# Reordering the second layer of a two-layer decoder step: memory attention first, one state tile for each pair of heads, eleven gate blocks last

## The chip, the cores and the metric

The kernel runs on one core of one Trainium2 chip. The metric is the device time of one execution in microseconds. Engines are named as in the profile: PE is the matrix engine (PEld its weight loads), DVE the vector engine, ACT the scalar engine, POOL and SP issue transfers.

## What is computed

One inference step of two layers for 256 prompt tokens and 8 sample tokens (264 columns), model width 2048. Each layer has one input projection that feeds a token mixer, four memory-attention heads and a gate; then an output projection and a LayerNorm.

```python
# layer 1: sliding-window attention; layer 2: HGRN2 recurrence, 12 heads of 128 x 128
fg = lb + (1 - lb) * sigmoid(f); qh = silu(q); kh = 1 - fg; vh = iv
o, s_new = hgrn2_chunked(qh, kh, vh, log(fg), s0)     # prompt: s0 = 0; samples: s0 = state_hgrn
o = o * rsqrt(mean(o*o, -1) + eps) * norm_w
mem_o = softmax(mq @ mk.T * 128**-0.5) @ mv           # 256 memory rows; samples have their own cached mk, mv
branch = concat([o, mem_o], -1) * silu(g)
x = LN(alpha * x + branch @ w_out)
# outputs: y of both groups, memory keys and values, window caches, final states (prompt and sample)
```

## The kernel before, in words

Everything that is streamed comes as blocks of 128x2048 numbers in f32 (1 MB): a projection's 2048x128 weight block, a memory cache of two samples, a state. `Stream` holds a list of units, one for each block, in an order written out in the code. A block is loaded by SP into a tile `raw` (four buffers), split by ACT (high f16 part, line 97) and DVE (low f16 part, line 98) into a tile `hl` (four buffers), up to three units ahead of its use, and then used by PE. `proj` multiplies a block in 48 passes: for each of 16 chunks high by high, high by low, low by high (`passes`, lines 303 to 305), into one of two PSUM banks `pj`. Smaller products use two banks `pt`, two `sc`, one `pv`, one `ms`.

In the second layer the units of a pair of heads `pi` are f, f, v, v, then for each head q, the head's state (512 KB, `state_unit`) and, for heads 0 to 7, its gate. After the twelve heads come the four memory queries `mq`, the eight memory caches (`ck_unit`, `cv_unit`) in turn with gates 8 to 13, gates 14 and 15, and sixteen blocks of the output projection (`o`). Gates of heads 0 to 7 (`early_gate`) wait in `mix` for their head; the others (`gate_unit`) are finished by `gate_fin` two gates later.

The prompt side of a pair is a generator, `hg_side`, of ten steps: seven levels of products (`hs`), each prepared by ACT and DVE, then the transposed keys (`pk` to `kn`), the states (`pu` to `s1`, `s2`), the outputs (`hpo` to `osb`), squares, `rms`, logarithm, exponential, and the scaling into `mix`. Pair n+1 uses the same buffers `st` and `prod` as pair n. `pump(1)` after every unit runs one step of the generator at the head of a queue; `drain()` ahead of the output projection runs what is left.

`state_unit` reads the split state for the eight samples (`hos`), then updates the f32 state in place in its `raw` tile: for each sample ACT scales (`raw <- raw, fg`, line 1237), PE spreads the value row over the partitions (`vb`, two `pt` banks of four samples each, from `vr` and a selector), DVE adds the product with the key column (line 1238); POOL writes the tile out.

The order in which each engine executes is fixed when the program is built: a scheduler puts every instruction into its engine's list by a timeline of its own, preferring what was written first. On the chip each engine takes its list from the top.

Of the kernel before, what the change touches and what calls it, by code (L numbers as in the profile page):

```python
# [21 lines left out]
TS = 8  # L22
# [11 lines left out]
NG1 = 8  # L34
# [12 lines left out]
LEVELS = (1, 2, 4, 8, 16, 32, 64)  # L47
NMASK = (len(LEVELS) - 1) * 64
# [9 lines left out]
class Stream:  # L58


    def __init__(self, nc, pool, nraw, nsplit):
        self.nc, self.pool = nc, pool
        self.nraw, self.nsplit = nraw, nsplit
        self.units = []
        self.raw = {}
        self.hl = {}

# [37 lines left out]
    def run(self, pump):  # L105
# [11 lines left out]
        for i in range(n):  # L117
# [8 lines left out]
            while free < prepped and (free <= i or self.units[free][5]):  # L126
                free += 1
# [7 lines left out]
def trunk_kernel(  # L135
# [75 lines left out]
    bias_s = pm.tile([P, 2, NQ], F32, name="bias_s")  # L211

# [94 lines left out]
    def proj(hl, src, n, name, cols=slice(None), tag="pj"):  # L307
# [77 lines left out]
    def q_unit(j):  # L385
        def fn(hl):
            load_bias(j)
            load_bias(j + 1)
            pt = proj(hl, xhl, T, f"q{j}")
# [326 lines left out]

    fin = {0: deque(), 1: deque()}
# [14 lines left out]
    def silu2(out, pt):  # L732
        nc.scalar.activation(out, pt, AF.Tanh, scale=0.5 * CP)
        nc.vector.scalar_tensor_tensor(out, out, 1.0, pt, op0=ALU.add, op1=ALU.mult)
# [10 lines left out]
    def residual(l, i, cols, n, pt):  # L745
        z = xres[:, i, cols]
        summed = nc.vector.scalar_tensor_tensor(z, z, ALPHA / CP, pt, op0=ALU.mult, op1=ALU.add)  # L747
# [235 lines left out]
    def f_unit(h):  # L983
        def fn(hl):
# [4 lines left out]
            pt = proj(hl, xhl, T, f"f{h}")  # L989
            i = h % 2  # L990
            if i == 0:
# [3 lines left out]
                cur["ks8"] = p1.tile([P, 2, TS], F32, tag="ks8", name=f"ks8{h}", bufs=2)  # L995
            fg, kk, ks8 = cur["fg"][:, i], cur["kk"][:, i], cur["ks8"][:, i]
# [6 lines left out]
            nc.vector.tensor_scalar_mul(ks8, kk, 1.0 / (SA * SK))  # L1003
# [5 lines left out]
    def hq_unit(h):  # L1009
        def fn(hl):  # L1010
# [5 lines left out]
            if h % 2 == 1:  # L1016
                side.append(hg_side(h // 2, cur["q"], cur["vn"], cur["fg"], cur["qk"]))
# [3 lines left out]
    later, due = [], []  # L1021

    def hv_unit(h):
        def fn(hl):
# [3 lines left out]
            if i == 0:  # L1028
                cur["vn"] = p1.tile([P, 2, 2, P], F32, tag="vn", name=f"vn{h}", bufs=2)
                cur["vr"] = p1.tile([P, 2, P], F16, tag="vr", name=f"vr{h}", bufs=2)  # L1030
# [10 lines left out]
    def hv_rows(h, vt, vs, vn, vr):  # L1041
# [7 lines left out]
        nc.vector.tensor_copy(vr[:, i], p16)  # L1049
# [14 lines left out]
    def hg_side(pi, q, vn, fg, qk):  # L1064
# [119 lines left out]
        for i, sq in enumerate(sqs):  # L1184
# [3 lines left out]
            scaled = mix[:, h] if h >= NG1 else sq  # L1188
# [3 lines left out]
            if h < NG1:  # L1192
# [4 lines left out]
    def state_unit(h):  # L1197
        def fn(hl):
            p1 = H["p"]
            pi, i = h // 2, h % 2  # L1200
            raw = stream.raw[state_at[h]][:, : TS * P]
            R = raw.rearrange("p (b v) -> p b v", b=TS)
            v = hl[:, :, : TS * P].rearrange("p s (b v) -> p s b v", b=TS)
            vr, fgs, ks8 = cur["vr"][:, i], cur["fg"][:, i, TP:T], cur["ks8"][:, i]
            qs, vts = (cur[n][:, i, TP:T] for n in ("q", "vt"))
            ks = cur["kk"][:, i]
            if i == 0:
                osb[pi] = p1.tile([P, 2, T], F32, tag="osb", name=f"osb{pi}", bufs=2)
            qk = p1.tile([P, TS], F32, tag="qk", name=f"qk{h}", bufs=2)
            qf = p1.tile([P, TS], F32, tag="qf", name=f"qf{h}", bufs=2)  # L1210
            qfh = p1.tile([P, TS, 2], F16, tag="qfh", name=f"qfh{h}", bufs=2)
            nc.vector.scalar_tensor_tensor(qf, qs, SA * 0.5 * CP, fgs, op0=ALU.mult, op1=ALU.mult)
            nc.vector.scalar_tensor_tensor(qk, qs, 8.0 * 0.5 * CP / SK, ks, op0=ALU.mult, op1=ALU.mult)
            qkh = p1.tile([P, 2, TS], F16, tag="qkh", name=f"qkh{h}", bufs=2)
            nc.scalar.activation(qkh[:, 0], qk, AF.Copy)
            nc.vector.tensor_tensor(qkh[:, 1], qk, qkh[:, 0], op=ALU.subtract)
            nc.scalar.activation(qfh[:, :, 0], qf, AF.Copy)
            nc.vector.tensor_tensor(qfh[:, :, 1], qf, qfh[:, :, 0], op=ALU.subtract)
            po = bank("ms", 1, f"hos{h}")
            pov = po[:, : 2 * TS].rearrange("p (b s) -> p b s", s=2)  # L1220
            for b in range(TS):
                mm(pov[:, b], v[:, 0, b], qfh[:, b], start=True, stop=False)
                mm(pov[:, b, 0:1], v[:, 1, b], qfh[:, b, 0:1], start=False, stop=True)
            pq = po[:, 2 * TS : 3 * TS]
            for s in range(2):
                mm(pq, H["ones"], qkh[:, s], start=s == 0, stop=s == 1)
            nc.vector.tensor_reduce(qf, pov, axis=AX.X, op=ALU.add)
            nc.vector.tensor_tensor(qk, pq, vts, op=ALU.mult)
            nc.vector.scalar_tensor_tensor(osb[pi][:, i, TP:T], qf, 1.0 / (SA * SA), qk, op0=ALU.mult, op1=ALU.add)
            for g in range(2):  # L1230
                pvb = bank("pt", 2, f"vb{h}{g}")
                for bb in range(4):
                    mm(pvb[:, bb * P : (bb + 1) * P], H["sel"][:, 4 * g + bb], vr, start=True, stop=True)
                for bb in range(4):
                    b = 4 * g + bb
                    s = R[:, b]
                    nc.scalar.activation(s, s, AF.Copy, scale=fgs[:, b : b + 1])
                    nc.vector.scalar_tensor_tensor(
                        s, pvb[:, bb * P : (bb + 1) * P], ks8[:, b : b + 1], s, op0=ALU.mult, op1=ALU.add
                    )  # L1240
# [192 lines left out]
```

## Time and profile before

| | |
|---|---|
| time, median of 3 runs | 906.81 us (906.51 to 907.01) |
| the profiled execution | 906.08 us, of which the span from first to last instruction is 904.3 us |
| PE busy | 886.6 us of the span (98%) |
| DVE, ACT busy | 701.5 us (78%), 582.4 us (64%) |
| granted PE clock, mean | 0.994 |
| second layer | from 420 us (first pass of `f`) to the end |

A row of a timeline gives the start, the duration, engine, line, operation, output <- inputs, shape, the number of such instructions, and in brackets how long the engine was idle before and what ended that. A row of a table of windows gives busy time (and count) of PE, PEld, DVE, ACT and POOL, the granted PE clock, and the share and rate of the transfers. A grouped row ends with busy time of the group, mean ns of one, and idle time before. PE's passes overlap in the records: one of 264 columns lasts 0.28 us and the next starts 0.11 us later.

### The profile page before, as it was taken

The page shows a single profiled execution, that of the slowest core. Times are in us where ns is not written, and L with a number is a line of the kernel's source. Part 1 is how long each engine was busy: PE and PEld are TensorE (multiplying, and loading weights), DVE is VectorE, ACT ScalarE, POOL GpSimd, SP SyncE. Part 2 cuts the span into 40 slices and gives each one's busy share as a digit, 9 for nine tenths or more (in the row PEclk, how much of TensorE's full clock was granted, in tenths as well). Part 3 has the DMA queues.
Part 4 walks back from the last instruction along what each step waited for, and adds up shares of the span by engine and source line. Part 5 has one row for each costly group of instructions (what it writes and reads, how often), then busy time and mean ns, then how long its engine had stood idle before and what let it go on. Part 6 is the DMA issues. An engine that isn't in the chain of part 4 may idle for free.

```text
span 904.3 us, 21814 instructions
## 1 busy us (share of the span) xinstructions
PE 886.6 (98%) x9281; PEld 762.9 (84%) x9281; DVE 701.5 (78%) x1230; ACT 582.4 (64%) x982; POOL 34.9 (4%) x68
## 2 busy tenths in 40 slices
PE   9999999999999999999999999999999999799996
PEld 6888889678888888876888888898888888688996
DVE  6879877669886666697687887979788989678736
ACT  6767776657664444476766877777777585858415
POOL 1100010000000000002000000000000000000000
PEclk9999999999999999999999999999999999899999
DMA  9998566557785555556374655827454878456303
GB/s 340 392 353 317 188 245 209 188 208 265 262 333 192 187 192 203 207 198 214 127 292 137 216 201 174 299 101 260 160 215 164 303 283 308 172 207 244 130 2 97
DMA packets 37853, 198.67 MB, mean 220 GB/s; under 512 B 4555, under 2 KB 10732, under 8 KB 17532
## 3 DMA queue, kind: packets, MB, share of 16 engines
q1 hardware_dynamic: 33024, 181.55, 56.3%
q0 software_dynamic: 4688, 15.67, 4.6%
q8 instruction: 72, 1.18, 0.5%
q14 instruction: 25, 0.20, 0.1%
q10 hardware_dynamic: 44, 0.07, 0.0%
HBM read 180.03 MB, written 17.22 MB: 218 GB/s over the span
## 4 chain that ended last, share of the span: by engine, by line
PE 77%; DVE 8%; ACT 6%; DMA 6%; issue 3%; SPq 0%; ACTq 0%; DVEq 0%
PE o L303 5%; PE o L305 5%; PE o L304 5%; PE g L305 5%; PE g L303 5%; PE g L304 5%; DVE hl L98 4%; ACT hl L97 2%; PE hv L305 2%; PE hv L303 2%; PE hv L304 2%; DMA raw<-in_w_in 2%; PE hq L303 2%; PE hq L305 2%; PE hq L304 2%
## 5 line engine op out<-in xcount | busy, mean ns | idle before, releaser
L98 DVE SCALAR_TENSOR_TENSOR hl<-raw,hl 128x2048 f16<-128x2048 f32 (+2 forms) x168 | 358.6, 2138 | 82.0 <-ACT hl L97 81.0
L97 ACT ACTIVATE hl<-raw 128x2048 f16<-128x2048 f32 (+2 forms) x168 | 299.2, 1784 | 97.8 <-PE o L305 45.4
L305 PEld LDWEIGHTS <-hl 128*128 128x128 f16 (+2 forms) x2048 | 197.4, 98 | 31.8 <-DVE hl L98 2.9
L303 PEld LDWEIGHTS <-hl 128*128 128x128 f16 (+2 forms) x2048 | 197.3, 98 | 30.6 <-issue 2.2
L304 PEld LDWEIGHTS <-hl 128*128 128x128 f16 (+2 forms) x2048 | 197.4, 98 | 30.3 <-issue 2.2
L305 PE MATMUL g<-xhl,hl 128*128 128x264 f16 x512 | 142.0, 277 | 2.4 <-DVE hl L98 2.4
L303 PE MATMUL g<-xhl,hl 128*128 128x264 f16 x512 | 141.9, 277 | 0.0
L304 PE MATMUL g<-xhl,hl 128*128 128x264 f16 x512 | 141.9, 277 | 0.0
L303 PE MATMUL o<-mix,hl 128*128 128x264 f16 x384 | 105.4, 276 | 0.8 <-DVE xres L747 0.8
L304 PE MATMUL o<-mix,hl 128*128 128x264 f16 x384 | 105.8, 276 | 0.0
L305 PE MATMUL o<-mix,hl 128*128 128x264 f16 x384 | 105.7, 276 | 0.0
L303 PE MATMUL q<-xhl,hl 128*128 128x264 f16 x192 | 53.0, 276 | 1.0 <-DVE kst L251 1.0
L303 PE MATMUL f<-xhl,hl 128*128 128x264 f16 x192 | 52.9, 276 | 0.4 <-DVE mvhl L251 0.4
L305 PE MATMUL hv<-xhl,hl 128*128 128x264 f16 x192 | 53.0, 276 | 0.0
L303 PE MATMUL hq<-xhl,hl 128*128 128x264 f16 x192 | 53.0, 276 | 0.0
L304 PE MATMUL hq<-xhl,hl 128*128 128x264 f16 x192 | 53.0, 276 | 0.0
L305 PE MATMUL hq<-xhl,hl 128*128 128x264 f16 x192 | 53.0, 276 | 0.0
L304 PE MATMUL hv<-xhl,hl 128*128 128x264 f16 x192 | 53.0, 276 | 0.0
L303 PE MATMUL hv<-xhl,hl 128*128 128x264 f16 x192 | 53.0, 276 | 0.0
L304 PE MATMUL q<-xhl,hl 128*128 128x264 f16 x192 | 53.0, 276 | 0.0
L305 PE MATMUL q<-xhl,hl 128*128 128x264 f16 x192 | 53.0, 276 | 0.0
L304 PE MATMUL f<-xhl,hl 128*128 128x264 f16 x192 | 52.9, 276 | 0.0
(338 smaller groups left out, 1858.4 us busy)
## 6 DMA issues: line engine op xcount, KB each, us to landing
raw<-in_w_in SPq DMA_DIRECT2D x88, 1024.0 KB, 6.4
raw<-in_w_o SPq DMA_DIRECT2D x32, 1024.0 KB, 5.0
raw<-in_w_mk SPq DMA_DIRECT2D x8, 1024.0 KB, 4.9
raw<-in_w_mv SPq DMA_DIRECT2D x8, 1024.0 KB, 4.9
raw<-in_c_mk SPq DMA_DIRECT2D x8, 1024.0 KB, 5.1
raw<-in_c_mv SPq DMA_DIRECT2D x8, 1024.0 KB, 7.0
raw<-in_state SPq DMA_DIRECT2D x12, 512.0 KB, 5.4
out_ss<-raw POOLq DMA_DIRECT2D x12, 512.0 KB, 5.5
```

The lines of the kernel that those rows point to most:

```text
L97: hi = self.nc.scalar.activation(hl[:, 0, s], raw[:, s], AF.Copy, scale=scale)
L98: lo = self.nc.vector.scalar_tensor_tensor(hl[:, 1, s], raw[:, s], scale, hl[:, 0, s], op0=ALU.mult, op1=ALU.subtract)
L303: mm(out, lhs(0), rhs(0), start=start, stop=False)
L304: mm(out, lhs(0), rhs(1), start=False, stop=False)
L305: return mm(out, lhs(1), rhs(0), start=False, stop=stop)
```

## The change

1. The order of the second layer's units is written out anew: f of head 0, the four `mq`, then the eight caches between the f, v, q and gate blocks of heads 0 to 3; pairs 2 to 5 follow; gates 0, 1, 2, 4, 6 are early (`EARLY`), and the other eleven stand last, 10 and 11 at their end, ahead of the output projection.
2. A pair's two states come as one block of 1 MB, with one set of the small sample operations for both heads (16 columns where there were 8). The pair's second update is put off to the unit after (`later`). The block's `raw` buffer is held until both are written out (`longer`).
3. `pumps` gives how many steps of a generator run after each unit: 0, 1 or 2.
4. The factor 1/(SA SK) moves into the selector constant, and the twelve small multiplications for `ks8` go.
5. The first projection of each layer (`q0`, `f0`) goes to the bank `pv`, high parts of all chunks first (`apart`).

`LATER` is empty, so that the code for updates during the output projection does nothing.

```diff
-NG1 = 8
+EARLY = (0, 1, 2, 4, 6)
+LATER = ()
...
-            while free < prepped and (free <= i or self.units[free][5]):
+            while free < prepped and (free + self.longer.get(free, 0) <= i or self.units[free][5]):
...
+        if apart:
+            pt = bank("pv", 1, name)
+            for k, (c, s, r) in enumerate([(c, 0, r) for c in range(NC) for r in range(2)] + [(c, 1, 0) for c in range(NC)]):
+                mm(pt[:, :n], w[:, s, c], src[:, r, c, cols], start=k == 0, stop=k == 3 * NC - 1)
+            return pt[:, :n]
...
-            nc.vector.tensor_scalar_mul(ks8, kk, 1.0 / (SA * SK))
...
+    def update(h, R, vr, fgs, ks, sel):
+        for g in range(2):
+            pvb = bank("pt", 2, f"vb{h}{g}")
+            for bb in range(4):
+                mm(pvb[:, bb * P : (bb + 1) * P], sel[:, 4 * g + bb], vr, start=True, stop=True)
+            for bb in range(4):
+                b = 4 * g + bb
+                s = R[:, b]
+                nc.scalar.activation(s, s, AF.Copy, scale=fgs[:, b : b + 1])
+                nc.vector.scalar_tensor_tensor(
+                    s, pvb[:, bb * P : (bb + 1) * P], ks[:, b : b + 1], s, op0=ALU.mult, op1=ALU.add
+                )
...
-    def state_unit(h):
+    def state_unit(pi):
...
+            half(0)
+            later.append(lambda: half(1))
...
+    for pi in range(2, HD // 2):
+        gated = 2 * pi - 2 in EARLY
+        f_of(2 * pi, 2)
+        f_of(2 * pi + 1, 1 if gated else 2)
+        v_of(2 * pi, 2)
+        v_of(2 * pi + 1, 2)
+        q_of(2 * pi)
+        q_of(2 * pi + 1)
+        state_of(pi)
+        if 2 * pi in EARLY:
+            gate_of(2 * pi)
...
-        pump(1)
+        pump(pumps.get(i, 1))
```

What this does to the engines' lists is shown at three places. In the names, `hl128` is the split block of unit 128 and the last group of digits is only a serial number; `hv9` is the v projection of head 9, `kn2`, `pu2`, `s12`, `osb2`, `hpo2` belong to pair 2, `vb60` and `vb61` are the two banks of head 6's update, `hvp6` and `hvr6` transpose its value rows, `g16` is gate 6 and `o10` output block 0 of the second layer.

The first place is where pair 2's prompt side ends while the next units run. ACT before:

```order
L1154 ACTIVATE kn2_8219<-pk2_8214 128x512
L1046 ACTIVATE vn6_8108<-hvp6_8221 128x256
L733 ACTIVATE hqs6_8280<-hq6_8231 128x264
L97 ACTIVATE hl118_8301<-raw118_7995 128x1024
L1217 ACTIVATE qfh6_8307<-qf6_8306 128x8
L1162 ACTIVATE s12_8288<-pu2_8283 128x256
L1215 ACTIVATE qkh6_8310<-qk6_8305 128x8
L1237 ACTIVATE raw118_7995<-raw118_7995,fg6_7951 128x128 x6
L1046 ACTIVATE vn6_8108<-hvp7_8294 128x256
L1237 ACTIVATE raw118_7995<-raw118_7995,fg6_7951 128x128 x2
L1173 ACTIVATE osb2_7517<-hpo2_8370 128x2x256
```

ACT at the same steps now:

```order
L1163 ACTIVATE kn2_8652<-pk2_8647 128x512
L1214 ACTIVATE raw131_9084<-raw131_9084,fg8_9140 128x128 x16
L1171 ACTIVATE s12_8714<-pu2_8709 128x256
L1055 ACTIVATE vn6_8596<-hvp6_8732 128x256
L100 ACTIVATE hl132_9443<-raw132_9089 128x2048
L1182 ACTIVATE osb2_8184<-hpo2_8720 128x2x256
L1010 ACTIVATE qk32_8_9141<-th8_9143,hl_lb_88 128x256
L1010 ACTIVATE qk32_8_9141<-th9_9237,hl_lb_88 128x256
L1055 ACTIVATE vn6_8596<-hvp7_8807 128x256
L1043 ACTIVATE hvt8_9302<-hv8_9251 128x264
L253 ACTIVATE vs0_5659<-hv8_9251 128x8
```

All sixteen scalings of the next pair's state now stand between `kn2` and `s12`, where there were eight in two pieces behind `s12`, and the reading of `hv8` out of its `pj` bank stands after them.

PE at this place before (the two `hpo2` that need no `s12`, with a gate block behind them):

```order
L305 MATMUL hq6_8231<-xhl_93,hl114_7992 128x264
L1169 MATMUL hpo2_8370<-st2_7719,vn4_7321 128x128
L1048 LDWEIGHTS vs0_5659
L1048 MATMUL hvr6_8225<-ident16_68,vs0_5659 128x128
L1158 MATMUL pu2_8283<-vn4_7321,kn2_8219 128x128 x4
L1170 MATMUL hpo2_8370<-st2_7719,vn4_7321 128x128
L303 LDWEIGHTS hl116_8145
L303 MATMUL g16_8385<-xhl_93,hl116_8145 128x264
```

PE now, from the last pass of `hv9` to the first of `hq8`:

```order
L309 MATMUL hv9_9361<-xhl_93,hl128_9086 128x264
L1180 MATMUL hpo2_8720<-qk32_4_7733,s12_8714 128x128
...
L1057 MATMUL hvr6_8736<-ident16_68,vs0_5659 128x128
L1054 MATMUL hvp7_8807<-ident_66,hvt6_8598 128x128 x2
...
L1057 MATMUL hvr7_8811<-ident16_68,vs1_5660 128x128
...
L1210 MATMUL vb60_8937<-vr6_8597,sel_t_5651 128x128
...
L1210 MATMUL vb61_8950<-vr6_8597,sel_t_5651 128x128
...
L1191 MATMUL rms20_8794<-osq20_8728,ones_rms_81 128x264
L1191 MATMUL rms21_8797<-osq21_8730,ones_rms_81 128x264
...
L1210 MATMUL vb70_9054<-vr6_8597,sel_t_5651 128x128
...
L307 MATMUL hq8_9446<-xhl_93,hl129_9183 128x264
```

Between two projections PE now has only short products that each wait for ACT or DVE, and no pass of a block among them.

The second place is the same step of pair 3. ACT before:

```order
L1154 ACTIVATE kn3_9006<-pk3_9001 128x512
L1046 ACTIVATE vn8_8895<-hvp8_9008 128x256
L1237 ACTIVATE raw127_8687<-raw127_8687,fg8_8738 128x128 x8
L733 ACTIVATE hqs8_9067<-hq8_9018 128x264
L97 ACTIVATE hl128_9088<-raw128_8782 128x2048
L1162 ACTIVATE s13_9075<-pu3_9070 128x256
```

ACT now:

```order
L1163 ACTIVATE kn3_9356<-pk3_9351 128x512
L100 ACTIVATE hl138_10006<-raw138_9731 128x2048
L1171 ACTIVATE s13_9418<-pu3_9413 128x256
L1055 ACTIVATE vn8_9300<-hvp8_9436 128x256
L1214 ACTIVATE raw138_9731<-raw138_9731,fg10_9717 128x128 x16
L1182 ACTIVATE osb3_8888<-hpo3_9424 128x2x256
L1010 ACTIVATE qk32_10_9718<-th10_9720,hl_lb_88 128x256
L1010 ACTIVATE qk32_10_9718<-th11_9854,hl_lb_88 128x256
L1055 ACTIVATE vn8_9300<-hvp9_9511 128x256
L1043 ACTIVATE hvt10_9950<-hv10_9899 128x264
L253 ACTIVATE vs0_5659<-hv10_9899 128x8
```

Sixteen scalings stand ahead of the reading of `hv10` out of its bank, which `hq10` needs next.

The third place is the end of the last pair's prompt side. PE before:

```order
L305 MATMUL hs5_64_10507<-qk16_2_5655 128x64
L1152 MATMUL pk5_10521<-ident_66,qk32_10_9379 128x128 x4
L1169 MATMUL hpo5_10636<-st5_10088,vn10_9535 128x128
L1170 MATMUL hpo5_10636<-st5_10088,vn10_9535 128x128
L1158 MATMUL pu5_10565<-vn10_9535,kn5_10526 128x128 x4
L666 MATMUL mrow1_10687<-ident_66,mst1_10685 32x128 x2
L1171 MATMUL hpo5_10636<-qk32_10_9379,s15_10570 128x128
...
L677 MATMUL mback1_10698<-ident_66,mrows1_10690 128x32 x2
L1182 MATMUL rms50_10704<-osq50_10644,ones_rms_81 128x264
L1182 MATMUL rms51_10707<-osq51_10646,ones_rms_81 128x264
L696 LDWEIGHTS hl148_10576
L696 MATMUL mso1_10796<-msphl1_10701,hl148_10576 128x2
```

PE now:

```order
L309 MATMUL hs5_64_10803<-qk16_2_5655 128x64
L1161 MATMUL pk5_10817<-ident_66,qk32_10_9718 128x128 x4
L1167 MATMUL pu5_10884<-vn10_9948,kn5_10822 128x128 x4
L1178 MATMUL hpo5_10955<-st5_10217,vn10_9948 128x128
L1179 MATMUL hpo5_10955<-st5_10217,vn10_9948 128x128
L1180 MATMUL hpo5_10955<-qk32_10_9718,s15_10889 128x128
...
L1191 MATMUL rms50_11027<-osq50_10963,ones_rms_81 128x264
L1191 MATMUL rms51_11030<-osq51_10965,ones_rms_81 128x264
L307 LDWEIGHTS hl150_10967
L307 MATMUL o10_0_11170<-mix_95,hl150_10967 128x264
L307 LDWEIGHTS hl151_11037
L307 MATMUL o11_0_11228<-mix_95,hl151_11037 128x264
```

The chain stood ahead of the caches' value products and two gates; it now stands behind all gates and behind 30 of the 48 passes of `o10` and of `o11`, and what follows it are the passes of these two that need heads 10 and 11.

More of the change, by code (lines that the diff above doesn't have):

```diff
@@ L1215, in fn @@
[L1215 to L1223, printed above, removed]
@@ L1225, in fn @@
+            pq = po[:, 4 * TS : 6 * TS]
             for s in range(2):
-                mm(pq, H["ones"], qkh[:, s], start=s == 0, stop=s == 1)
+                mm(pq, H["ones"], qkh[:, s].rearrange("p i b -> p (i b)"), start=s == 0, stop=s == 1)
             nc.vector.tensor_reduce(qf, pov, axis=AX.X, op=ALU.add)
[L1228 to L1240, printed above, removed]
@@ L1269, in trunk_kernel, with f_of, v_of, q_of @@
[L1269 to L1274 removed]
+    def f_of(h, n=1):
+        w1("f", h, f_unit(h), n)
+    def v_of(h, n=1):
+        w1("v", h, hv_unit(h), n)
+    def q_of(h, n=1):
+        w1("q", h, hq_unit(h), n)
+    f_of(0)
```

186 lines of the change are left out of this document (132 added, 54 removed).

## The prediction

> **What bounds the kernel now.** I read the page's first part, then the table of 20 us windows, then 2 us windows where PE is not full, then the timelines of each engine there. The page first.
>
> ```profile
> span 904.3 us, 21814 instructions
> PE 886.6 (98%) x9281; PEld 762.9 (84%) x9281; DVE 701.5 (78%) x1230; ACT 582.4 (64%) x982; POOL 34.9 (4%) x68
> ```
>
> PE is the bound: anything gained must come from its 2% of idle time or from its clock. The 20 us windows of the second layer say where these are.
>
> ```profile
> 740.00:760.00 20.00, 20.00 (x248) 17.69 (x247) 20.00 (x23) 14.40 (x14) 0.00 (x0) 1.00 0.91 327
> 760.00:780.00 20.00, 16.23 (x184) 13.44 (x182) 13.03 (x20) 11.82 (x19) 0.54 (x1) 0.95 0.66 240
> 780.00:800.00 20.00, 18.27 (x211) 15.25 (x210) 19.67 (x34) 15.73 (x30) 0.00 (x0) 0.88 0.58 220
> 800.00:820.00 20.00, 19.70 (x176) 17.12 (x175) 12.37 (x19) 12.12 (x18) 0.00 (x0) 1.00 0.30 103
> ```
>
> The second column is PE: full at 740, then idle for 3.77, 1.73 and 0.30 us, 5.8 together. Two windows also have a granted clock under 1, which loses 0.05 x 20 and 0.12 x 20, 3.4 us. So one place in the layer is worth 9.2 us. In 2 us steps:
>
> ```profile
> 774.00:776.00 2.00, 1.01 (x9) 0.74 (x7) 0.86 (x5) 1.50 (x5) 0.54 (x1) 1.00 0.72 176
> 776.00:778.00 2.00, 1.86 (x34) 1.57 (x34) 0.23 (x1) 1.97 (x4) 0.00 (x0) 1.00 0.95 393
> 778.00:780.00 2.00, 1.76 (x19) 1.31 (x19) 0.00 (x0) 1.97 (x4) 0.00 (x0) 0.53 0.05 21
> 780.00:782.00 2.00, 2.00 (x41) 1.68 (x40) 1.67 (x4) 2.00 (x3) 0.00 (x0) 0.61 0.03 8
> 784.00:786.00 2.00, 0.56 (x3) 0.43 (x4) 2.00 (x5) 2.00 (x3) 0.00 (x0) 0.74 0.00 0
> 786.00:788.00 2.00, 2.00 (x11) 1.36 (x10) 2.00 (x1) 2.00 (x6) 0.00 (x0) 0.50 0.64 201
> ```
>
> Half clock follows an idle stretch and lasts between 3 and 4 us each time (778 to 782, 784 to 788), so one such spell costs about 1.7 us of work. What PE waits for is the end of pair 5's prompt side. Its steps in the timelines of PE, ACT and DVE:
>
> ```profile
> 769.31 0.63 PE L1152 MATMUL pk<-ident,qk 128*128 128x128 f32 x4
> 771.47 0.49 PE L1169 MATMUL hpo<-st,vn 128*128 128x128 f32 x2 [1.53 <-ACT st L1147]
> 772.02 1.09 PE L1158 MATMUL pu<-vn,kn 128*128 128x128 f32 x8
> 773.58 0.49 PE L1171 MATMUL hpo<-qk,s 128*128 128x128 f32 x2 [0.26 <-ACT s L1162]
> 776.01 1.16 PE L1182 MATMUL rms<-osq,ones_rms 128*128 128x264 f32 x4
> 785.43 0.40 PE L305 MATMUL g<-xhl,hl 128*128 128x264 f16 x1 [1.73 <-DVE hl L98]
> ```
>
> ```profile
> 769.24 1.91 ACT L97 ACTIVATE hl<-raw 128x2048 f16<-128x2048 f32 x1 [3.84 <-issue]
> 771.32 0.58 ACT L1154 ACTIVATE kn<-pk 128x512 f32<-128x512 f32 x1
> 773.15 0.38 ACT L1162 ACTIVATE s<-pu 128x256 f32<-128x256 f32 x1 [1.25 <-PE pu L1158]
> 774.93 0.57 ACT L1173 ACTIVATE osb<-hpo 128x512 f32<-128x512 f32 x1
> 775.53 0.73 ACT L1177 ACTIVATE osq<-osb 128x264 f32<-128x264 f32 x2
> 776.41 1.28 ACT L1183 ACT_TABLE_LOAD   x1
> 777.71 0.85 ACT L1183 ACTIVATE osq<-rms,eps_rms 128x264 f32<-128x264 f32 x2
> 778.58 1.28 ACT L1186 ACT_TABLE_LOAD   x1
> 779.87 0.73 ACT L1186 ACTIVATE osq<-osq 128x264 f32<-128x264 f32 x2
> 782.31 0.41 ACT L729 ACTIVATE mix<-sil 128x264 f16<-128x264 f32 x1
> ```
>
> ```profile
> 780.33 0.90 DVE L1189 SCALAR_TENSOR_TENSOR mix<-osb,small_t,osq 128x264 f32<-128x264 f32 x2 [3.67 <-ACT osq L1186]
> 781.74 0.77 DVE L728 SCALAR_TENSOR_TENSOR sil<-sil,mix 128x264 f32<-128x264 f32 x2
> ```
>
> From the end of `pk` to a finished head is a chain of 12 us that jumps between engines, and PE has about 3 us of it. The first layer's list is unchanged but for `q0`.
>
> **The change part by part.** Every block of 48 passes stays, so PE's work is the same; I count only idle time and clock.
>
> *The first projections in `pv`.* The rows of both places:
>
> ```profile
> 30.50 0.27 PE L303 MATMUL q<-xhl,hl 128*128 128x264 f16 x1 [1.00 <-DVE kst L251]
> 420.09 0.27 PE L303 MATMUL f<-xhl,hl 128*128 128x264 f16 x1 [0.43 <-DVE mvhl L251]
> 424.93 0.28 PE L304 MATMUL f<-xhl,hl 128*128 128x264 f16 x1
> ```
>
> High parts first lets PE start without the low part, and another bank takes away the wait for the read-out: 1.0 and 0.4 us. Bounds 0 and 1.4; I take the rows, -1.4. The last two rows are 44 passes after the first: 4.84 us, 0.11 each, 5.4 a block.
>
> *The old hole.* Pair 5's chain leaves 770 and the caches' products run beside blocks in layer two's first third: -9.2. It is 0 at the least, if the caches bring a hole along.
>
> *The new tail.* Now the whole chain stands behind 30 of 48 passes of `o10` and of `o11`; both `pj` banks are taken, so nothing else can run on PE from the end of `pk5`. Its length, from the rows above: kn 0.58, pu 1.09, s 0.38, hpo 0.49, osb 0.57, osq 0.73, table 1.28 (rms lies beside it), logarithm 0.85, table 1.28, exponential 0.73, scaling 0.90, half of the gate product 0.39, high part 0.41: 9.7 us, and some 0.08 for each of eight handovers (osq ends at 776.26, the table load starts at 776.41), so 10.3. PE works in it for pu 1.09, hpo 0.49 twice, rms 1.16: 3.2. Idle 7.1 us; 6.5 if handovers cost nothing, 8.5 if the readers of `hs5_64` are late too. Idle time as in the rows of 774 and 784 was followed by half clock; I take one spell, discounted for what still waits, 1.5 (0.5 to 3, up to two spells).
>
> *Pair 2's end at `hq8`.* ACT's list has sixteen scalings between `kn2` and `s12`. Durations:
>
> ```profile
> 536.08 2.44 ACT L1237 ACTIVATE raw<-raw,fg 128x128 f32<-128x128 f32 x8
> 538.41 0.62 ACT L1079 ACTIVATE qk<-qk 128x512 f16<-128x512 f32 x1
> L98 DVE SCALAR_TENSOR_TENSOR hl<-raw,hl 128x2048 f16<-128x2048 f32 x64 | 146.6, 2292 | 21.2 <-ACT hl L97 20.8
> L97 ACT ACTIVATE hl<-raw 128x2048 f16<-128x2048 f32 x64 | 121.9, 1905 | 21.9 <-DMA raw<-in_w_in 6.7 <-PE g L305 5.3 <-issue 3.8
> L1237 ACT ACTIVATE raw<-raw,fg 128x128 f32<-128x128 f32 x96 | 29.5, 391 | 3.5 <-DVE hl L98 3.5
> L1034 ACT ACTIVATE hvt<-hv 128x264 f32<-128x264 f32 x12 | 4.5, 379 | 6.8 <-PE hv L305 6.8
> L1046 ACT ACTIVATE vn<-hvp 128x256 f32<-128x256 f32 x12 | 4.5, 377 | 0.0
> ```
>
> Eight scalings last 2.33 us up to the next row, sixteen 4.7. From the end of `pk2`, `s12` is ready at 0.1 + 0.6 + 4.7 + 0.4 = 5.8 (7.0 if the scalings first wait for the low split, as the row of L1237 shows). PE has 31 passes of `hv9` (3.5) and 1.5 of small products: it stands at 5.0, idle for 0.9 to 2.1. Behind `s12` ACT has vn 0.38, the split of `hl132` 1.9, osb 0.57, two `qk32` at 0.59 (row of kn's width), vn 0.38, `hvt8` 0.38 and `vs0` 0.2, 5.0 us; with the low half of `vs0` on DVE behind it and two handovers to PE, 6.1 until `hq8` can have `hv8`'s bank. PE has 2.8 in this (twelve `vb` at 0.11, half of the rms row 0.6, four `hpo`, two `hvr` and one `hvp` with some 0.9): idle 3.3. Together 4.2 to 5.4, taken 4.8, and less than a spell of half clock, 1.5 (0 to 2.5). This holds DVE's low split of `hl132` (2.29) too, ahead of the updates that free the `vb` banks; it lies beside ACT's list.
>
> *Pair 3's end at `hq10`.* From the end of `pk3`: kn 0.6, split 1.9, then its low half 2.29 before the scalings may overwrite `raw`, scalings 4.7, osb 0.57, two `qk32` 1.2, vn 0.38, `hvt10` 0.38, `vs0` 0.2: 12.2, with handovers 12.7. PE has 58 passes (6.5) and 3.7 of small products (sixteen `vb` 1.8, pu 1.09, hpo, hvp and hvr some 0.8): 10.2. Idle 2.5 (1.8 to 4.5, the latter if DVE runs a split ahead of the updates), clock 0.8 (0 to 1.7).
>
> *The rest.* At `hq6` the same pattern has more passes behind it: 0.3 (0 to 1). One set of sample operations takes twelve small multiplications off DVE, and tiny products off PE, which has cover for the others: 0 (down to -0.5). The state tiles come as one load of 1 MB where there were two of 512 KB, and stores the same bytes; loads queued on SP behind a held `raw` come later, but the 740 row has the transfers at 0.91 and PE full: nothing, with up to a block of 5.4 for each load that comes late.
>
> Sum: -1.4 - 9.2 + (7.1 + 1.5) + (4.8 + 1.5) + (2.5 + 0.8) + 0.3 = +7.9. The profiled execution took 906.1, so 914.0. That execution is 0.7 us under the median of the runs, less than the terms are known to; 914 stands. With all lower bounds (6.5 + 0.5, 4.2, 1.8, -0.5 for the rest) it would be 908.0, with all upper ones 925; such sums rarely meet, and the case's own range is 908 to 921.
>
> The row of 776 bears on the clock terms: PE was busy for 1.86 of 2 us, yet the next row has 0.53. [...]
>
> **The rivals.**
> 1. *Three bare places, as summed*: 914. For it speaks that each rests on the lists as they will run and on durations of the trace.
> 2. *ACT runs ahead, and only the tail is bare.* The scalings of `raw131` need only the loaded state and its split; if ACT reaches them while PE is still a block behind, they are done before `kn2` is due, and `hvt8` right after `hv8`. For it: ACT is busy 64% of the span. Against it: `kn2` stands ahead of them in the list, so they can't start before it. Then -10.6 + 8.6 = -2.0 and about 904. It decides if ACT's list from `kn` to `hvt` is under 5 us rather than 10 to 12.
> 3. *The tail is covered as well*, if pair 5's chain ends before `o10` is due: -10.6 and 895.5. Against it: PE's own list has `hs5_64` and `pk5` behind those 30 passes.
> 4. *State tiles starve the loads*, or the early caches bring their own hole: `raw` has four buffers, two can be held by a state in update. Two late loads of 5.4 us give 914 + 10.8, about 925; one 919. For it: the 740 row's 0.91; against it the second row's 0.66 and the third's 0.58.
>
> **How the numbers follow.** About 0.2%, 1.8 us, is what a measurement of this kernel can tell from no change. Chances: the first 0.66 (of which 0.05 lies within 1.8 us of before), the second 0.16 (its 904 is 0.3% under, so 0.10 faster and 0.06 same), the third 0.06, the fourth 0.12. Slower is 0.61 + 0.12 = 0.73, same 0.11, faster 0.16. The range reaches from the second case, 904, over the first to one late load more, 922: it leaves out the third, and about half of the fourth.
>
> **What would show it.** The profile of the changed kernel should have no idle time from 420 to 425; PE idle ahead of the last `hpo2` (ended by ACT's `s`), ahead of `vb61` and `vb70`, and ahead of `hq8`, 4 to 5 us together; 2 to 3 ahead of `hq10`; and between `pk5` and the last 18 passes of `o10` 7 us, ended step by step by ACT, with half clock behind it. The idle time ended by `mback` and by the split's DVE part should be gone. I am wrong if ACT's scalings are done before `pk2` ends, if PE shows blocks ahead of `vb60`, or if the sum of idle time in layer two stays under 10 us.

## The result and the profile after

The changed kernel takes 919.0 us (median of 4 runs, 916.96 to 920.58) where the kernel before took 906.9: a ratio of 1.0133, 95% interval 1.0108 to 1.0157. It is slower, as forecast, and inside the range given; 914 was 5 us too low. One run below lies apart from the rest of its kernel (926.1 us of the order alone, against 910.5 to 918.0); it is left out of that kernel's median and interval, and that kernel's only profile is of this run. The profiled execution of the changed kernel took 920.58 us. Its page begins:

```profile
span 918.8 us, 21686 instructions
PE 889.7 (97%) x9269; PEld 762.3 (83%) x9269; DVE 695.4 (76%) x1170; ACT 582.1 (63%) x964; POOL 35.1 (4%) x68
```

PE has 12 products fewer and 3.1 us more busy time; its idle time grew from 17.7 us (904.3 less 886.6) to 29.1. The two make up the 14.5 us between the spans. Where the idle time lies, in the main windows of 20 us that are not full or whose granted clock is under 1, with that of 760 beside them (columns as before):

```profile
40.00:60.00 20.00, 18.65 (x168) 15.75 (x165) 15.84 (x22) 12.39 (x15) 1.71 (x2) 1.00 0.98 356
520.00:540.00 20.00, 19.16 (x196) 16.26 (x195) 16.30 (x18) 17.22 (x33) 0.00 (x0) 1.00 0.61 211
660.00:680.00 20.00, 15.86 (x147) 13.38 (x146) 13.18 (x38) 15.58 (x38) 1.18 (x3) 1.00 0.25 94
680.00:700.00 20.00, 19.33 (x242) 16.66 (x240) 19.17 (x32) 13.46 (x19) 0.43 (x1) 1.00 0.59 201
700.00:720.00 20.00, 17.63 (x160) 15.15 (x158) 13.94 (x34) 15.51 (x36) 1.19 (x3) 0.93 0.46 176
720.00:740.00 20.00, 20.00 (x199) 17.22 (x198) 14.90 (x23) 12.26 (x18) 0.42 (x1) 0.98 0.53 188
760.00:780.00 20.00, 20.00 (x194) 17.73 (x192) 13.33 (x31) 12.97 (x22) 1.08 (x2) 1.00 0.40 142
780.00:800.00 20.00, 18.08 (x179) 15.67 (x178) 19.11 (x33) 9.94 (x13) 0.53 (x1) 1.00 0.73 259
800.00:820.00 20.00, 16.82 (x171) 14.29 (x170) 10.98 (x15) 9.30 (x15) 0.55 (x1) 0.99 0.39 143
820.00:840.00 20.00, 16.29 (x133) 13.59 (x133) 12.21 (x16) 13.16 (x15) 0.00 (x0) 0.84 0.31 104
```

The row of 760 is full: the old hole is gone. In its place stand the three bare places of the prediction: 4.14 us at 660 (`hq8`), 2.37 at 700 (`hq10`) and 6.9 at 800 and 820 (the tail). The longest of PE's waits there, from its timeline, end with `s12` behind the scalings, with the read-out of the transposed values (`vn`) and with the update in `raw`, which free a `pt` bank for `vb`, and at the end with the scaled heads. None stands ahead of `hq8` or `hq10` itself.

```profile
666.22 0.49 PE L1180 MATMUL hpo<-qk,s 128*128 128x128 f32 x2 [1.63 <-ACT s L1171]
670.02 0.38 PE L1210 MATMUL vb<-vr,sel_t 128*128 128x128 f16 x4 [1.33 <-ACT vn L1055]
715.71 0.38 PE L1210 MATMUL vb<-vr,sel_t 128*128 128x128 f16 x4 [1.22 <-DVE raw L1215]
817.76 1.16 PE L1191 MATMUL rms<-osq,ones_rms 128*128 128x264 f32 x4 [1.14 <-ACT osq L1186]
823.71 0.60 PE L307 MATMUL o<-mix,hl 128*128 128x264 f16 x2 [4.78 <-ACT mix L739]
```

ACT's timeline at the first place, where the scalings start as soon as DVE has written the low half and hold `s` back until 665.81:

```profile
659.59 0.60 ACT L1163 ACTIVATE kn<-pk 128x512 f32<-128x512 f32 x1
661.12 4.78 ACT L1214 ACTIVATE raw<-raw,fg 128x128 f32<-128x128 f32 x16 [0.94 <-DVE hl L101]
665.81 0.36 ACT L1171 ACTIVATE s<-pu 128x256 f32<-128x256 f32 x1
666.07 0.36 ACT L1055 ACTIVATE vn<-hvp 128x256 f32<-128x256 f32 x1
666.34 1.90 ACT L100 ACTIVATE hl<-raw 128x2048 f16<-128x2048 f32 x1
```

Two waits were not forecast. A gate block at 787 waits for DVE, which runs a whole low split (2.28 us) ahead of the product that frees a `pj` bank; and in layer one, where the wait at `q0` is gone, another query block waits 18 us later:

```profile
787.29 0.27 PE L307 MATMUL g<-xhl,hl 128*128 128x264 f16 x1 [1.92 <-DVE sil L744]
48.62 0.29 PE L307 MATMUL q<-xhl,hl 128*128 128x264 f16 x1 [1.20 <-DVE qss L255]
```

### The profile page after: what moved, and what is told of

Its sections match the earlier page's. It is cut to its first block, busy times and chain, and to the rows that moved or that the text cites. A ratio compares the mean times of both kernels' runs of the same rounds, so it can differ in the third digit from the quotient of the medians.

```text
span 918.8 us, 21686 instructions
## 1 busy us (share of the span) xinstructions
PE 889.7 (97%) x9269; PEld 762.3 (83%) x9269; DVE 695.4 (76%) x1170; ACT 582.1 (63%) x964; POOL 35.1 (4%) x68
## 4 chain that ended last, share of the span: by engine, by line
PE 72%; ACT 10%; DVE 9%; DMA 7%; issue 2%; SPq 0%; ACTq 0%; DVEq 0%
PE g L307 6%; PE g L308 6%; PE g L309 6%; PE o L307 5%; PE o L309 5%; PE o L308 5%; DVE hl L101 4%; DMA raw<-in_w_in 3%; ACT hl L100 3%; ACT raw L1214 2%; PE f L308 2%; PE f L309 2%; PE f L307 2%; PE mk L308 2%; PE mk L309 2%
## 5 line engine op out<-in xcount | busy, mean ns | idle before, releaser
L100 ACT ACTIVATE hl<-raw 128x2048 f16<-128x2048 f32 (+2 forms) x162 | 298.0, 1843 | 94.3 <-PE o L309 47.6
L307 PEld LDWEIGHTS <-hl 128*128 128x128 f16 (+2 forms) x2016 | 194.4, 98 | 35.8 <-issue 6.0
L308 PEld LDWEIGHTS <-hl 128*128 128x128 f16 (+2 forms) x2016 | 194.6, 98 | 31.6 <-issue 3.7
L309 PEld LDWEIGHTS <-hl 128*128 128x128 f16 (+2 forms) x2016 | 194.6, 98 | 28.3 <-issue 0.2
L307 PE MATMUL hq<-xhl,hl 128*128 128x264 f16 x192 | 53.7, 280 | 0.1
L308 PE MATMUL hq<-xhl,hl 128*128 128x264 f16 x192 | 53.7, 280 | 0.0
L309 PE MATMUL hq<-xhl,hl 128*128 128x264 f16 x192 | 53.6, 279 | 0.0
L307 PE MATMUL q<-xhl,hl 128*128 128x264 f16 x176 | 48.6, 276 | 1.2 <-DVE qss L255 1.2
L308 PE MATMUL q<-xhl,hl 128*128 128x264 f16 x176 | 48.6, 276 | 0.0
L309 PE MATMUL q<-xhl,hl 128*128 128x264 f16 x176 | 48.6, 276 | 0.0
L309 PE MATMUL f<-xhl,hl 128*128 128x264 f16 x176 | 48.6, 276 | 0.0
L308 PE MATMUL f<-xhl,hl 128*128 128x264 f16 x176 | 48.6, 276 | 0.0
```

Of the source, the lines that this page charges most:

```text
L100: hi = self.nc.scalar.activation(hl[:, 0, s], raw[:, s], AF.Copy, scale=scale)
L307: mm(out, lhs(0), rhs(0), start=start, stop=False)
L308: mm(out, lhs(0), rhs(1), start=False, stop=False)
L309: return mm(out, lhs(1), rhs(0), start=False, stop=stop)
```

## The experiments

The question was whether the three places are three costs, each with its own cause, or one. Times below are medians; ratios are to the kernel before on the same chip; the edits are given in short.

**The order alone.** The kernel before with the new order and step numbers, but each head's state behind its own q, as it was:

```
+EARLY = (0, 1, 2, 4, 6)
 f_of(0); four mq; caches between f, v, q, gates of heads 0 to 3
+    q_of(2 * pi);     state1_of(2 * pi)
+    q_of(2 * pi + 1); state1_of(2 * pi + 1)
+    pump(pumps.get(i, 1))
```

> The kernel before with the new order of units and the new numbers of steps alone; each head keeps its own state tile, directly behind its q. Theory A (the tail and the two bare places come from the pair's state tile with its sixteen scalings in one piece; the order alone only removes the old hole): in this kernel's lists the last prompt side ends beside gates 10 and 11, so the idle time after pk5 is under 1 us, the hole of 9.2 us is gone, and the time is 906.9 - 9.2 = 898, 896 to 901. Rival B (memory first delays the six prompt sides, which run one after the other, so that the tail comes with the order): idle time of 5 us or more after pk5, 904 to 908.

913.0 us, ratio 1.0080 (1.0055 to 1.0105). Theory A falls: without the state tile the order still costs more than the hole that it removes. Rival B falls as well: the time is above its 908, and the wait behind the last side is 2.0 us where it asked for 5. The bare places at `hq8` and `hq10` are gone, but PE now waits elsewhere. Its list of waits from 420 us on (what waited, for what, us in total, times, longest):

```profile
PE hd L1120 <- ACT osq L1183: 10.3, 4, 3.6
PE o L303 <- ACT mix L729: 2.0, 1, 2.0
PE hv L303 <- ACT th L998: 1.3, 1, 1.3
```

`hd`, the next pair's first product, takes the `sc` bank that `rms` of the pair before has just filled, and stands a dozen passes behind it in PE's list; ACT still has a table load and two logarithms to do (1.28 and 0.85 us in the rows of before). The sizes are those of the run of 926.1 us; what they are in a run of 913 isn't known.

**The scalings later.**

```
+    marks["tanh"] = nc.scalar.activation(out, pt, AF.Tanh, ...)      # in silu2
+    with tc.issue_after(behind.ins):       # behind: tanh of the pair's second q
         nc.scalar.activation(s, s, AF.Copy, scale=fgs[:, b : b + 1])
```

> The changed kernel, where the sixteen scalings of a state may only be issued behind the tanh of the pair's second q, so that they stand ahead of neither s12 nor hvt10. Theory A: at hq8 the idle time falls from 4.9 us to 2 to 3 (the split of hl132 and the read-out still stand in a row), at hq10 from 2.7 us to under 1, and the spell of half clock behind it (1.7 us) goes; the tail stays. 919 - 2.5 - 2 - 1.7 = 913, 911 to 916. Rival B (the scalings only move, and what waits for the state's buffer is late instead): 919 or more, with new idle time in the rows behind hq9 and hq11.

915.7 us, 1.0119 (1.0091 to 1.0148). Its list of waits:

```profile
PE hd L1129 <- ACT osq L1192: 2.7, 2, 2.4
PE vb L1210 <- ACT vn L1055: 1.6, 1, 1.6
PE hvp L1054 <- DVE s L1173: 1.4, 1, 1.4
PE hpo L1180 <- ACT s L1171: 0.7, 1, 0.7
```

The wait for `s12` is gone (the 0.7 us is the same wait of pair 3, at the second place), but PE still stands at both places, for `vn` at the first and for DVE (`s`) at the second, and `hd` has become a new wait. The time is 3.3 us under 919 and inside theory A's range, but the intervals of the two kernels overlap, and theory A's account holds in part only: the mean granted clock of the profiled execution is 0.993, as in the changed kernel, so that a spell of half clock less does not show, and the second place, which was to fall under 1 us, has 2.7 us of idle time in its row of 700.

**Cover for the tail.**

```
-        for c in range(NC):                         # output blocks of layer two
+        for c in [c for c in range(NC) if c not in (10, 11)] + [10, 11]:
+    out_part(..., tag={2: "ms", 3: "pt"}.get(i, "pj"))
```

> The changed kernel, where the output blocks take heads 10 and 11 last, and output blocks 2 and 3 use the banks ms and pt, so that 91 passes (10.2 us) stand between pk5 and the first pass that needs heads 10 and 11. Theory A (the tail is a chain without cover): idle time after pk5 falls from 7.6 us to under 1, no half clock there (1.5 us): 919 - 9 = 910, 908 to 912. Rival B (the splits of blocks 12 and 13 on ACT and DVE push the chain back by their own 1.9 and 2.3 us): half the gain, 914 to 916.

915.9 us, 1.0111 (1.0096 to 1.0126): 3.1 us under 919, a third of theory A's 9 and within rival B's range. Its waits around the tail:

```profile
PE o L307 <- ACT hl L100: 2.7, 2, 1.4
PE o L307 <- ACT mix L740: 2.2, 1, 2.2
```

The last `rms` starts at 822.2 us where it started at 818.5: PE now puts passes between the steps of the chain, which waits for PE in its turn (ACT stands 3.2 us each for `pu` and for `hpo`, where it stood 1.0 and 1.3). And four output blocks in work hold all four `hl` buffers, so the split of the fifth starts only when the first block is done, and PE waits 2.7 us for it. Neither theory had that second mechanism; the size is rival B's.

**Both.**

> Both edits together, the late scalings and the cover of the tail. Theory A (the places are independent): the sum of the two gains, 919 - 6 - 9 = 904, 901 to 908. Rival B (what is taken away at one place is waited for at the next): less than the larger of the two gains, 909 or more.

915.2 us, 1.0105 (1.0076 to 1.0133). Theory A's 904 is out, and rival B's 909 or more holds. Each edit alone came out 3 us under 919 and both together 4, but the intervals of the four kernels overlap (that of the changed kernel is 1.0108 to 1.0157), so these runs do not show whether gains as small as these add up.

**Another bank for the second rms**, on the order alone and on the changed kernel:

```
-            pm = bank("sc", 2, f"rms{pi}{i}")
+            pm = bank("sc", 2, f"rms{pi}{i}") if i == 0 else bank("ms", 1, f"rms{pi}{i}")
```

> The kernel with memory first and a state tile for each head, where the second rms of a pair takes the bank ms instead of sc, so that the first product of the next pair (hd) has a bank that nobody reads. Theory C (with the new order PE's list has hd close behind rms, and it waits there for the logarithm that reads the rms bank: 10.3 us in four waits, and half clock behind them): these waits go, the time falls by 8 to 14 us to 899 to 905. Rival D (what PE waits for is the prompt side's own length; hd starts earlier, and hs waits for ACT and DVE instead): within 2 us of 912.

> The changed kernel with that edit alone. In its lists each prompt side starts between the two rms of the one before, the last one ends beside gate 10, and no product of it stands behind the passes of o10. Theory C (the tail stands there because the six prompt sides run one after the other through the same banks, and each begins only when the one before has been read out): the tail's 7.6 us and its half clock (1.5) go, 919 - 9 = 910, 908 to 912, with bare places still beside the pair's updates. Rival D: the freed time is waited for at hs and at the updates, 915 or more.

930.6 us, 1.0253 (1.0227 to 1.0278), and 923.0 us, 1.0163 (1.0139 to 1.0188). Theory C's times fail twice; rival D's 915 or more holds for the second kernel, and its 912 for the first is far off too. The tail of the changed kernel is indeed gone, and so are the waits of `hd`; in their place `hs` waits for ACT's preparation in the second kernel, 10.0 us in nine waits, and `hq` for the read-out of a value block in both. The first kernel's list:

```profile
PE hq L303 <- DVE vs L251: 11.6, 3, 4.5
PE g L303 <- DVE sil L734: 2.9, 1, 2.9
PE hs L303 <- ACT qk L1079: 2.8, 5, 1.1
```

**The old order with the state tile.**

```
     for pi in range(HD // 2):
         f, f, v, v, q, q, state_of(pi), two early gates for pi < 4
     four mq; eight caches in turn with gates 8 to 13; gates 14, 15
```

> The changed kernel with the units of layer two in the order of before (memory queries and caches behind the twelve heads, gates 0 to 7 early, one step after each unit but two after a state), but with the state tile of a pair. Theory A (state tile makes the bare places; the order moves the hole): the hole of 9.2 us is back near the caches, the tail is gone (in the lists the last scaling has gates 14 and 15 behind it), 1 to 3 places with bare updates: 919 - 9.1 + 9.2 - 2 = 917, 912 to 919. Rival B (all that is lost comes with the order): within 2 us of 906.9.

913.7 us, 1.0070 (1.0047 to 1.0093), inside theory A's range; the hole is back and the tail is gone, as it said, but its bare places are not there. From 420 to 760 us PE is full to within 0.3 us, with sixteen scalings for a pair: the state tile does not make bare places by itself. All that is lost lies in the old hole, which has become larger (11.4 us idle where it was 5.5, and clocks of 0.74 and 0.83 where they were 0.95 and 0.88):

```profile
760.00:780.00 20.00, 12.80 (x116) 10.85 (x114) 12.79 (x19) 7.38 (x10) 0.00 (x0) 0.74 0.54 199
780.00:800.00 20.00, 15.78 (x213) 12.81 (x212) 14.76 (x26) 16.57 (x30) 0.55 (x1) 0.83 0.41 150
```

**The first projections alone**, on the kernel before (part 5 of the change as in its diff):

> The kernel before with the first projection of each layer in the bank pv, high parts first, and nothing else. As predicted: -1.4 us, 905.2 to 905.7. Rival (the wait of 1 us ahead of q0 comes back ahead of q2, as the profile of the changed kernel has it, 1.37 us ended by DVE's split of the second query block): within 0.5 us of 906.7.

905.8 us, 0.9988 (0.9972 to 1.0004), 1.2 us less than the 907.0 of before. The sign is that of the forecast, but the interval holds no change too; unclear. In its profile PE is full from 20 to 80 us, so that the wait ahead of another query block, which the changed kernel has at 48.62, does not come with this edit alone.

**One step after every unit**, on the changed kernel:

```
-        pump(pumps.get(i, 1))
+        pump(1)
```

> The changed kernel with one step of a prompt side after every unit, state units included, instead of steps dealt out by hand (0, 1 or 2). Its lists have passes of hq8 and hq9 between pu2, hpo2 and rms2, and passes of hq10, hq11 and gate 3 at the same steps of pair 3; but the last side's hs, pk, pu, hpo and rms all stand behind 30 passes of o10 and o11. Theory E (dealt by hand, pair 2's pk and pu are promised the pt banks ahead of pair 3's value rows, so that hvp6, and with it the read-out of hv8, waits for a side that runs a pair late): the idle time at hq8 (4.9), at hq10 (2.7) and the half clock there (1.7) go, the tail grows by 4 to 8 us: 919 - 9.3 + 6 = 916, 913 to 919, with less than 1.5 us idle from 655 to 725. Rival A (the state tile's scalings make those places): idle time of 4 us or more stays there, 922 or more.

919.3 us, 1.0139 (1.0118 to 1.0160). Its rows:

```profile
660.00:680.00 20.00, 20.00 (x195) 17.81 (x194) 13.43 (x33) 17.85 (x37) 1.07 (x2) 1.00 0.51 192
700.00:720.00 20.00, 20.00 (x198) 17.87 (x196) 15.41 (x25) 15.18 (x34) 0.54 (x1) 1.00 0.50 186
780.00:800.00 20.00, 15.91 (x138) 12.90 (x136) 14.30 (x27) 12.11 (x17) 0.55 (x1) 0.91 0.32 113
800.00:820.00 20.00, 10.45 (x99) 8.44 (x98) 8.40 (x18) 8.74 (x16) 0.54 (x1) 0.80 0.02 7
```

Both places are gone, scalings and all, as theory E said, and nothing was gained (its range ended at 919): PE reaches the output blocks at 785.5 us where it was 804.2, and then waits 13.6 us in the two windows from 780 to 820.

**Gates 3, 5 and 7 back between the pairs.**

```
-EARLY = (0, 1, 2, 4, 6)
+EARLY = tuple(range(8))        # two gates behind each of the first four pairs
```

> The changed kernel with gates 3, 5 and 7 back between the pairs (gates 0 to 7 early, eight gates last). Theory F (with fewer blocks between the pairs PE reaches the units of pair n+2 before the prompt side of pair n is read out; before, the first f of pair n+2 started 1 to 13 us behind rms of pair n, now 16 to 36 us ahead of it): the places at hq8 and hq10 go (9.3 us), the tail stays, hd waits some 1.5 us for each of four rms: 919 - 9.3 + 6 = 916, 912 to 918. Rival A (scalings): the places stay, 919 or more.

915.7 us, 1.0090 (1.0061 to 1.0119), the 916 of theory F, though not by its sum: `hd` waits 0.5 us in all where it had 1.5 at each of four `rms`, and `hs` waits 6.1 us in seven waits. Rows of 660 and 700 are full here too (20.00 and 20.00), and the tail has grown, 8.3 us idle with a clock of 0.61:

```profile
800.00:820.00 20.00, 11.72 (x87) 9.44 (x85) 7.70 (x17) 8.98 (x16) 0.54 (x1) 0.61 0.17 65
```

**hd behind the end of the pair before**, on the order alone, and then **all together** with the output blocks' new chunk order, block 2 in `ms` and the first projections in `pv`:

```
+    tc.add_manual_dep(hd, scaling that ends the pair before, order only)
```

> The kernel with memory first and a state tile for each head, where the first product of a pair (hd) is ordered behind the scaling that ends the pair before, so that some 19 passes of a block stand between rms and hd. Theory C (PE waits there for the logarithm): the four waits of 10.3 us and the half clock behind them go; the last side moves later by as much, with 3 to 5 us idle behind rms5: 912 - 12 + 4 = 904, 900 to 908. Rival D (the prompt side's own length is the limit, what is not waited for at hd is waited for at the end): 910 or more.

> The same kernel, and the output blocks with heads 10 and 11 last, output block 2 in bank ms, and the first projections in bank pv. 43 passes (4.8 us) stand behind rms5. Theory C: the idle time behind rms5 falls under 2 us, and 1 us of pv comes on top: 900, 897 to 904, faster than before. Rival D: 907 or more, the time lost at other places of the lists.

915.5 us, 1.0096 (1.0070 to 1.0121): the waits of `hd` are 0.4 us (10.3 in the run of 926.1 us without the edit) and nothing came of it, so theory C fails a third time and D holds. All together: 910.7 us, 1.0043 (1.0026 to 1.0059), the best of the new order and still slower than before, as rival D had it; from 780 to 840 us PE is full there. No kernel of this study is shown to be faster than the one before.

**What the traces have in common.** The six prompt sides use one `st` and one `prod`, and `pump` takes their steps from one queue, so they run one after the other. For `hd` and `rms` the profile gives the first and the last start; the first `hd` opens the first side, the last `rms` all but ends the sixth. In this order: before, after, one step each, gates back, all together.

```profile
L1120 PE MATMUL hd<-hqs,qk x48: 272/275/275, 459.3 to 731.3; 128*128 128x128 f32 x48
L1182 PE MATMUL rms<-osq,ones_rms x24: 386/386/490, 506.9 to 776.8; 128*128 128x264 f32 x24
```

```profile
L1129 PE MATMUL hd<-hqs,qk x48: 272/275/275, 491.1 to 773.6; 128*128 128x128 f32 x48
L1191 PE MATMUL rms<-osq,ones_rms x24: 386/386/490, 560.4 to 818.5; 128*128 128x264 f32 x24
```

```profile
L1191 PE MATMUL rms<-osq,ones_rms x24: 386/386/490, 556.1 to 815.3; 128*128 128x264 f32 x24
```

```profile
L1191 PE MATMUL rms<-osq,ones_rms x24: 386/386/806, 560.2 to 815.7; 128*128 128x264 f32 x24
```

```profile
L1195 PE MATMUL rms<-osq,ones_rms x24: 386/386/442, 552.6 to 811.0; 128*128 128x264 f32 x24
```

In the kernels with memory first, PE's list has the first `hd` of head 0 alone, 11 to 16 us ahead of that of head 1, which needs the pair's second q; before, the two lay 3 us apart. The rows of head 1, before and after:

```profile
462.59 0.61 PE L1120 MATMUL hd<-hqs,qk 128*128 128x128 f32 x4
503.16 0.61 PE L1129 MATMUL hd<-hqs,qk 128*128 128x128 f32 x4
```

So the table counts from head 1. Its three stretches (up to that `hd`, from there to the last `rms`, and behind) add up to the span by construction: they say where the time lies, not why.

| kernel | first `hd` of head 1 | last `rms` | between | span | span behind last `rms` |
|---|---|---|---|---|---|
| before | 462.6 | 776.8 | 314.2 | 904.3 | 127.5 |
| old order, state tile | 454.2 | 782.6 | 328.4 | 910.7 | 128.1 |
| after | 503.2 | 818.5 | 315.3 | 918.8 | 100.3 |
| scalings later | 500.9 | 813.0 | 312.1 | 913.9 | 100.9 |
| one step each | 500.0 | 815.3 | 315.3 | 916.1 | 100.8 |
| gates back | 503.2 | 815.7 | 312.5 | 915.6 | 99.9 |
| `hd` behind, heads' own states | 505.8 | 814.7 | 308.9 | 915.4 | 100.7 |
| cover for the tail | 500.8 | 822.2 | 321.4 | 914.4 | 92.2 |
| both | 501.0 | 822.8 | 321.8 | 917.1 | 94.3 |
| all together | 506.1 | 811.0 | 304.9 | 906.8 | 95.8 |

In these rows the six sides take 305 to 328 us, wherever PE waits meanwhile. In the changed kernel they start 40.6 us later and take 1.1 us more, while the stretch behind them shrinks by 27.2: together the 14.5 us between the spans. In the kernel before, four of the six sides start as their own second q ends; in the changed kernel sides 2 to 6 start 29 to 42 us behind theirs, but only 2 to 6 us behind the last `rms` of the side before, so there it is the sides that wait for each other. With the two places taken away they take as long (315.3 with one step each, 312.5 with gates back): PE reaches the tail earlier and waits there longer. In the old order the state tile makes the sides 14 us longer; they end 5.8 us later though they start 8.4 us sooner, and that is where the hole grows.

The account has its limits. All together has the earliest end of the sides in the new order, and more passes beside it, but there the end is no longer what costs: PE is full from 780 to 840 us, and the largest loss lies around the start of the first side, in two waits for the split of an `f` block and for ACT's `th`:

```profile
500.00:520.00 20.00, 16.15 (x199) 13.53 (x197) 18.17 (x29) 13.69 (x18) 0.54 (x1) 0.91 0.96 364
```

The two kernels with the other bank for `rms`, not in the table, end their sides at 812.0 (after) and 821.7 us and have 105.6 and 106.8 us behind that, which this account doesn't explain. Also not in it are the first projections alone, whose stretches are near those of before (314.1 between, 130.2 behind), and the order alone, whose profile is of the run of 926.1 us.

## Why the prediction was right, and where it was not

- **The hole.** -9.2 us: the row of 760 is full after. As said.
- **The tail.** Idle 7.1 forecast, 6.9 measured (0.94, 0.03, 1.14, 1.08, 2.00 and 1.71 in the six steps of 2 us from 812 to 824), and one spell of half clock, of which some 3 us had work in them, 1.5 us:

```profile
818.00:820.00 2.00, 0.92 (x4) 0.54 (x4) 0.00 (x0) 1.97 (x4) 0.00 (x0) 0.93 0.01 2
820.00:822.00 2.00, 0.00 (x0) 0.00 (x0) 0.04 (x1) 1.97 (x4) 0.00 (x0) 0.50 0.00 0
824.00:826.00 2.00, 2.00 (x11) 1.31 (x10) 0.47 (x2) 0.00 (x1) 0.00 (x0) 0.50 0.00 0
```

- **hq8.** Idle 4.8 forecast, 4.14 measured. The first part is as summed: 1.63 at `hpo` for `s12` (0.9 to 2.1 forecast). The second part, 3.3, was to end ahead of `hq8` with the read-out of `hv8`; PE waited 2.2 instead, at `vb` (0.31 and 1.33) and `rms` (0.60), and not at `hq8`. So the mechanism, ACT's list in its order, is right, the place of the second wait is not, and the closeness of the sum owes something to luck. The half clock of 1.5 did not come: the clock is 1.00 through the row of 660.
- **hq10.** Idle 2.5 forecast, 2.37 measured, again at `vb` (0.32, 1.22 and 0.84) and not at `hq10`; clock 0.8 forecast, 1.4 (0.07 x 20) and 0.4 (0.02 x 20) measured.
- **The rest.** 0.3 us forecast for `hq6` and nothing for all other places; this is the term that was most mis-sized. The rows of 520 (0.84), 680 (0.67) and 780 (1.92) with smaller ones hold some 4 us. The step that failed for 780 is the sentence that everything else has cover: DVE's list has a split (2.28 us) ahead of the product that frees PE's bank, and the prediction weighed only the lists near the three places.
- **The first projections.** -1.4 forecast. The waits at 30.5 and 420 are gone, but the row of 40 has 1.35 us idle that it had not before, so that next to nothing is left. With the edit alone the wait at 48.62 does not come; why it comes here is open.
- **PE's work.** "Every block of 48 passes stays, so PE's work is the same" is not borne out: PE is busy for 3.1 us more, and the spells of half clock cost about as much as before: some 6.2 us of PE's work ran in them (717.3 to 720.7, and 823.7 to 826.5 of the tail's), as in the kernel before (778.3 to 781.6 and 785.0 to 788.4). By the distance from each start to the next, the short products `vb`, `hvr`, `hvp` and `rms` take 1.9 us of it; the rest is spread.
- **The sum.** The profiled executions lie 14.5 us apart where +7.9 was forecast. Of the 6.6 us that are missing, about 3.7 are the rest, 1.4 the first projections and 3.2 PE's busy time beyond the clock, while the three places came out 1.5 lower than their terms. The upper sum of 925 doesn't come out of its terms: with the upper bounds of the places and of `hq6` beside -10.6 it is 922.1.
- **The sum as an account of cause.** The prediction added the places as if each were a price of its own. The idle times were near, the additivity was not: the kernel with one step each has neither of two of them and the same time; with gates back they are gone and the time is 3 us less, not 8. Rival 3 came nearest the true limit, the end of pair 5's chain against `o10`, but I weighed it only as cover for one place and did not ask when the first side starts.
- **The fourth rival** (loads starved by state tiles) did not show: no wait of PE in the second layer of the changed kernel is ended by a load.
- **The half clock.** The prediction lets it follow an idle stretch and last 3 to 4 us. In the changed kernel, by the clocks in the rows, one spell began at 717.3 us, where the longest wait before it was 1.22 us (rows below), and lasted 3.4 us; the tail's began at 819.7, only 0.8 us into the wait of 4.78, and lasted 6.8. At `hq8` none came, though PE stood for half of the time from 664 to 672. What decides between them isn't settled by these rows.

```profile
714.00:716.00 2.00, 0.67 (x8) 0.52 (x8) 1.19 (x5) 2.00 (x6) 0.00 (x0) 1.00 0.00 0
716.00:718.00 2.00, 1.16 (x12) 0.88 (x10) 1.86 (x8) 2.00 (x8) 0.44 (x1) 0.83 0.00 0
```

That the serial sides set the end of the changed kernel is argued from its waits and from the kernels in which places went and the sides stayed as long; no run moves the start of the first side alone, and in all together they no longer set it. What makes a side take some 50 us is not settled either: with one step each the sixth had its last `hd` at 790.3 and its last `rms` at 815.3, when PE had little else, so it isn't the work itself. Two causes remain: the one `st` and `prod`, and the queue, from which the changed kernel takes nine or ten steps for each of the later pairs whatever the buffers. A second `st` and `prod` would decide it; it was not run.

## What to carry to other kernels

Ahead of adding up idle places, look for a chain that runs through the whole stage on one buffer, and write down when it starts, how long it takes and what is left to do behind it: a change that delays its start may pay at its end, whatever it does to the places in between. A wait that is removed elsewhere may only move, as the two places here did; test that two fixes add up before believing in two causes. In a kernel whose lists are fixed when it is built, an edit that frees one bank may reorder all that follows: here one bank's change cost some 17 us in one kernel and, at the edge of the intervals, 4 in another.

## What the runs showed that was not expected

- More work in flight on PE can starve the splits: with four output blocks begun, all four `hl` buffers were held and PE waited 1.3 and 1.4 us for the next two.
- A product that waits for a PSUM bank read by the logarithm also waits for what ACT has ahead of it: in the run of 926.1 us the first `rms` starts at 559.5 us, the first logarithm only at 565.1, and `hd` waits 3.2 us there and 3.6 at the longest; the table load takes 1.28 us and the two logarithms 0.85 in the rows of before.
- The kernel before spread over 0.6 us in its first runs (906.51 to 907.09) and over 6.0 us beside a later group of kernels (904.62 to 910.64), so differences of 1 us, as that of the first projections, stay open even with twelve runs.
